# 24 of the 32 tiles of each up projection as seven block products, and plain f through DRAM

## The chip, the cores and the metric

The kernel runs on one core of one Trainium2 chip. The metric is device time in microseconds of one execution. A core has TensorE (PE, matmuls, with PEld loading its weights), VectorE (DVE), ScalarE (ACT), GpSimd (POOL) and SyncE (SP), which here only issues DMAs. Each works through its instructions in order and waits on semaphores. SBUF is the on-chip memory, PSUM holds what PE writes, and DRAM is reached by DMA.

## The reference

Two layers, each a token mixer (differential attention in layer 0, a gated short convolution in layer 1) and an MLP with squared ReLU, every part between two RMSNorms with gains, over 1024 tokens and 16 meta tokens of width 1024, in fp32. What the change touches is the MLP (D_MODEL 1024, D_FF 4096):

```python
def _sqrelu_mlp(h, w_up, w_down):
    a = jax.nn.relu(jnp.einsum('bld,df->blf', h, w_up))
    return jnp.einsum('blf,fd->bld', a * a, w_down)

def reference(...):
    ...
        hres = hres + _rmsnorm(m, norm_g[i, 1])
        h = _rmsnorm(hres, norm_g[i, 2])
        hres = hres + _rmsnorm(_sqrelu_mlp(h, w_up[i], w_down[i]), norm_g[i, 3])
    return hres[:, N_META:]
```

## The kernel before

Activations lie transposed: 128 features on the partitions, tokens along the row (1028 in layer 0, as four meta tokens are still needed there, and 1024 in layer 1). Every fp32 operand is split into a high part of reduced precision (`hi`, a cast on ACT) and the rest (`lo`, a subtraction on DVE), and every product is three matmuls: hi by hi, lo by hi, hi by lo. A weight tile of 128 outputs is one DMA of 512 KB into `w_raw`, then a cast and a subtraction of 128x1024 (`load_weights`, L149 and L150). With K = 1024 a tile takes 8 x 3 = 24 matmuls for each chunk of tokens (`product`, L187): three chunks of 340 to 344 in layer 0, two of 512 in layer 1.

The MLP of a layer runs in `mlp`. The first four up tiles (the head) run while the norm ahead of them is being finished: `norm_step` adds the residual into m (L389, L390), writes m to DRAM (L394), splits gain times m into H and L, and sums squares into ssn (ACT L211, POOL L212); a sum over the partitions on PE (L203) and `rsqrt_mean` then make the scale rs for each chunk. The up products run on the unscaled x and are scaled behind the ReLU (L456). Then come 24 tiles in twelve pairs (`up_pair`), and four plain tiles. f is the squared result. The down projection takes the 24 middle tiles of f by Strassen's scheme in Winograd's form: a 2 by 2 block product by seven products instead of eight. Its operand sums of f are made behind each pair (L486 to L489, on DVE), split, and written to `seven_dram` by two large DMAs (L494).

The head's f goes to `plain_dram` and comes back last. The last four plain tiles stay in SBUF in `stage`, and the down projection begins with them (`down_plain`, four weight tiles of two outputs each, ACT copying each result into acc). Meanwhile the first block of sums, fourteen loads of 514 KB, comes into the tiles that held H and L (the base load, L523). Then `Sevens.run` takes the seven products of each weight block in an order written out by hand for PE, three PSUM chains a, b and c, each product read out by a DVE add while the next ones run (L591, L614).

Only PE's order in the loops of seven is fixed by hand. Elsewhere the order on each engine and on SP's queue is made by a scheduler when the program is built, and then fixed. Tiles named by a tag share buffers: a new one waits until the old one's readers are done. The DMA semaphores are eight, used in turn, so that at most eight DMAs are under way. `wp` holds one `w_raw` and two pairs of hi and lo; `two` gives the two big tiles that hold v (a pair's f and sums) and later acc.

Of the kernel before, what the change touches and what calls it, by code (L numbers as in the profile page):

```python
# [16 lines left out]
F32 = mybir.dt.float32  # L17
F32R = mybir.dt.float32r
AF = mybir.ActivationFunctionType
ALU = mybir.AluOpType  # L20
# [62 lines left out]
def trunk(ctx: ExitStack, tc: tile.TileContext, xt, wall, gains, lam_p, subln, convw, out):  # L83
# [27 lines left out]
    plain_dram = [drp.tile([P, 2 * FB, w], F32, name=f"plain_dram{i}") for i, w in enumerate((T1, SEQ))]  # L111
# [335 lines left out]
    def up_product(fp, w, hi, lo, rs, cols, boundary=False):  # L447
        c0, n = cols
        ps = any_bank("up")[:, :n]
        if boundary:  # L450
            settle(0, cols)
        product(ps, w, hi, lo, 0, range(KC), cols)
        if boundary:
            settle(1, cols)
        r = fp.tile([P, n], F32, tag="r", name=f"r_{count[0]}", bufs=2)
        nc.vector.scalar_tensor_tensor(r, ps, 0.0, rs[:, c0 : c0 + n], ALU.max, ALU.mult)  # L456
        return r

    def up_plain(fp, hi, lo, rs, W, stage, groups, chunks, boundary=False):

        fh, fl = quarters(stage, W)
        for group in groups:
            ws = [weights() for _ in group]
            for cols in chunks:
                s = slice(cols[0], cols[0] + cols[1])
                for i, w in zip(group, ws):
                    r = up_product(fp, w, hi, lo, rs, cols, boundary)
                    nc.scalar.activation(r, r, AF.Square)
                    nc.vector.tensor_copy(fh[:, i, s], r)
                    nc.vector.tensor_sub(fl[:, i, s], r, fh[:, i, s].bitcast(F32))  # L470
                    spent(3 * KC, cols[1])

    def up_pair(fp, hi, lo, rs, H, t, chunks, stage, spool):

        v = flat(t)[:, : 8 * H].rearrange("p (a b) -> p a b", a=8)
        for e in range(2):
            w = weights()
            for cols in chunks:
                c0, n = cols
                r = up_product(fp, w, hi, lo, rs, cols)  # L480
                for z in range(2):
                    a, b = max(c0, z * H), min(c0 + n, (z + 1) * H)
                    if a < b:
                        nc.scalar.activation(v[:, SLOT[e, z], a - z * H : b - z * H], r[:, a - c0 : b - c0], AF.Square)
                spent(3 * KC, n)
        nc.vector.tensor_sub(v[:, 3], v[:, 7], v[:, 0])  # L486
        nc.vector.tensor_sub(v[:, 2], v[:, 5], v[:, 3])
        nc.vector.tensor_sub(v[:, 4], v[:, 5], v[:, 7])
        nc.vector.tensor_sub(v[:, 6], v[:, 1], v[:, 2])  # L489
        sv = stage[:, : 14 * H].rearrange("p (a b c) -> p a b c", a=7, b=2)  # L490
        for a, b in ((0, 4), (4, 7)):
            nc.scalar.copy(sv[:, a:b, 0], v[:, a:b])
            nc.vector.tensor_sub(sv[:, a:b, 1], v[:, a:b], sv[:, a:b, 0].bitcast(F32))
            nc.sync.dma_start(spool[:, a:b], sv[:, a:b].bitcast(F32))  # L494
# [150 lines left out]
    def mlp(layer, hi, lo, rs, H, two, base, base_plain, head, chunks, opened, psum_of, reopen):  # L645
# [3 lines left out]
        ff = ExitStack()  # L649
        fp = ff.enter_context(pool("ff", side="right"))  # L650

        def stage():
            return fp.tile([P, 2 * FB * W], F32R, tag="stage", name=f"stage{layer}_{count[0]}")

        st = stage()
        up_plain(fp, hi, lo, rs, W, st, [list(range(FB))], head, True)
        for i, f in enumerate(quarters(st, W)):
            nc.sync.dma_start(plain[:, i * FB : (i + 1) * FB], f.bitcast(F32))
# [739 lines left out]
```

## Time and profile before

| | us |
|---|---|
| time, median of 3 runs (lowest, highest) | 2402.52 (2401.92, 2403.31) |
| the profiled execution's own time | 2403.25 |
| its span | 2401.1 |
| granted TensorE clock over the span | 0.993 |
| PE without a matmul (span less busy) | 58.9 |
| layer 0: up from 606 to 980, plain down to 1025, down by sevens to 1265 | 374, 45, 240 |
| layer 1: up from 1689 to 2055, plain down to 2099, down by sevens to 2339 | 366, 44, 240 |

Matmuls overlap each other, so the length of one is more than its share of PE's time: 128x512 lasts 392 ns in the median while one starts every 229 ns. What a matmul costs is read from the pitch of a stretch, not from its duration.

### The profile page before, as it was taken

To read this page: it belongs to the slowest core of one execution; us is meant where nothing else is said; L and a number is where in the kernel's file an instruction comes from. 1 tells how busy PE (TensorE), PEld (TensorE's weight loads), DVE (VectorE), ACT (ScalarE), POOL (GpSimd) and SP (SyncE) were. 2 spreads that over 40 slices of the span, in tenths; PEclk is the share of its full clock that TensorE was granted. 3 is DMA by queue.
4 is the path that set the end of the run, shared out by engine and by line. 5 is a ranking of instruction groups with operands and counts; after the bars stand their busy time and mean duration, and the time that the engine had idled before them with its cause. 6 is when DMAs were issued, how large, how long until landed. Compare 5 with 4: busy or idle time off the path is not lost.

```text
span 2401.1 us, 36496 instructions
## 1 busy us (share of the span) xinstructions
PE 2342.2 (98%) x14330; PEld 2202.7 (92%) x14330; DVE 1485.9 (62%) x2663; ACT 996.4 (41%) x1901; POOL 445.3 (19%) x438
## 2 busy tenths in 40 slices
PE   8999999999999999999999999999999999999997
PEld 7899999999899999999999899999888888888886
DVE  7887777764954554367666944433954455277766
ACT  6777777765533333322224522224533333312224
POOL 3211111104400000033324200003400000133316
PEclk9999999999999999999999999999999999999998
DMA  4222222243355655475732411122355655477552
GB/s 136 58 63 62 63 63 63 74 144 113 108 212 203 234 190 207 176 291 206 270 136 97 139 45 47 51 68 61 119 219 202 228 218 185 177 288 261 214 200 71
DMA packets 109915, 357.66 MB, mean 149 GB/s; under 512 B 10928, under 2 KB 55344, under 8 KB 102576
## 3 DMA queue, kind: packets, MB, share of 16 engines
q1 hardware_dynamic: 109744, 355.33, 41.8%
q8 instruction: 113, 1.85, 0.3%
q14 instruction: 58, 0.48, 0.1%
HBM read 225.94 MB, written 120.84 MB: 144 GB/s over the span
## 4 chain that ended last, share of the span: by engine, by line
PE 81%; DVE 11%; ACT 3%; issue 2%; DMA 2%; SPq 0%; DVEq 0%; ACTq 0%
PE up L187 27%; PE pa L591 11%; PE dn L187 5%; PE pb L591 5%; PE mo L187 4%; PE bg L187 4%; PE ug L187 3%; PE cg L187 3%; PE pc L591 3%; PE po L1305 2%; DVE HL L392 2%; PE s L1219 1%; PE tr L1266 1%; PE s L1220 1%; PE q L972 1%
## 5 line engine op out<-in xcount | busy, mean ns | idle before, releaser
L187 PE MATMUL up<-HL,w_hi 128*128 128x344 f32 (+3 forms) x1312 | 453.8, 346 | 4.0 <-DVE HL L392 3.8
L187 PEld LDWEIGHTS up<-HL,w_hi 128*128 128x128 f32 x1312 | 247.0, 188 | 27.1 <-DVE HL L392 6.7
L150 DVE TENSOR_TENSOR w_lo<-w_raw,w_hi 128x1024 fp32r<-128x1024 f32 (+1 forms) x111 | 137.2, 1237 | 189.0 <-ACT w_hi L149 188.9
L456 DVE SCALAR_TENSOR_TENSOR r<-up,ssn 128x344 f32<-128x344 f32 (+3 forms) x164 | 93.5, 573 | 259.1 <-PE up L187 258.5
L149 ACT CAST w_hi<-w_raw 128x1024 fp32r<-128x1024 f32 (+2 forms) x135 | 140.3, 1040 | 260.2 <-PE up L187 153.5
L187 PE MATMUL up<-HH,w_hi 128*128 128x344 f32 (+1 forms) x768 | 246.0, 320 | 0.0
L187 PE MATMUL up<-HH,w_lo 128*128 128x344 f32 (+1 forms) x768 | 245.6, 321 | 0.0
L569 POOL TENSOR_TENSOR s_tmp<-w_raw 128x256 f32<-128x256 f32 x48 | 35.5, 739 | 1025.2 <-DMA w_raw<-in_wall 792.6
L187 PEld LDWEIGHTS up<-HH,w_lo 128*128 128x128 f32 x768 | 144.7, 189 | 0.5 <-issue 0.2
L187 PEld LDWEIGHTS up<-HH,w_hi 128*128 128x128 f32 x768 | 144.7, 188 | 0.2
L212 POOL TENSOR_TENSOR mss<-mss,sq 128x344 f32<-128x344 f32 (+2 forms) x42 | 50.1, 1198 | 375.8 <-ACT sq L211 366.8
L561 ACT CAST s_hi<-s_tmp 128x1024 fp32r<-128x1024 f32 x48 | 50.4, 1050 | 163.8 <-PE pb L591 147.0
L1229 ACT ACTIVATE E<-E,mn 16x16 f32<-16x16 f32 (+5 forms) x144 | 105.3, 732 | 23.9 <-DVE mn L1224 23.4
L187 PE MATMUL up<-YHb,w_hi 128*128 128x512 f32 (+2 forms) x272 | 103.6, 381 | 0.0
L187 PE MATMUL up<-YHa,w_lo 128*128 128x512 f32 (+2 forms) x272 | 103.6, 381 | 0.0
L187 PE MATMUL up<-YHb,w_lo 128*128 128x512 f32 (+2 forms) x272 | 103.5, 381 | 0.0
L187 PE MATMUL up<-YHa,w_hi 128*128 128x512 f32 (+2 forms) x272 | 103.4, 381 | 0.0
L187 PE MATMUL mo<-HL,w_hi 128*128 128x342 f32 (+2 forms) x312 | 99.9, 320 | 0.0
L150 POOL TENSOR_TENSOR w_lo<-w_raw,w_hi 128x1024 fp32r<-128x1024 f32 (+1 forms) x24 | 57.5, 2394 | 196.7 <-ACT w_hi L149 174.1
L1224 DVE CUSTOM_DVE_ANT_0 E<-s,G 16x16 f32<-16x16 f32 (+5 forms) x144 | 64.4, 455 | 39.9 <-PE s L1220 37.4
L614 DVE TENSOR_TENSOR acc<-acc,pa 128x512 f32<-128x512 f32 x96 | 65.8, 687 | 33.6 <-PE pa L591 32.0
L561 ACT CAST a_hi<-w_raw 128x512 fp32r<-128x512 f32 x48 | 29.8, 620 | 134.2 <-DMA w_raw<-in_wall 126.8
(501 smaller groups left out, 7291.4 us busy)
## 6 DMA issues: line engine op xcount, KB each, us to landing
w_raw<-in_wall SPq DMA_DIRECT2D x189, 512.0 KB, 3.7
seven_dram<-stage SPq DMA_DIRECT2D x12, 2056.0 KB, 6.3
seven_dram<-stage SPq DMA_DIRECT2D x12, 2048.0 KB, 6.3
fx<-seven_dram SPq DMA_DIRECT2D x42, 514.0 KB, 7.0
fx<-seven_dram SPq DMA_DIRECT2D x42, 512.0 KB, 6.9
seven_dram<-stage SPq DMA_DIRECT2D x12, 1542.0 KB, 9.3
seven_dram<-stage SPq DMA_DIRECT2D x12, 1536.0 KB, 8.7
HL<-seven_dram SPq DMA_DIRECT2D x21, 514.0 KB, 7.4
```

Source lines behind the costliest of these rows:

```text
L149: nc.scalar.copy(hi_part, raw[:, cols])
L150: (eng or nc.vector).tensor_sub(lo_part, raw[:, cols], hi_part.bitcast(F32))
L187: nc.tensor.matmul(ps, lhs[:, a:b], rhs(k, cols), start=n == 0, stop=n == last)
L212: (eng or nc.gpsimd).tensor_add(ss, ss, sq)
L392: nc.vector.scalar_tensor_tensor(row(L, c, s), mc, gn, hc.bitcast(F32), ALU.mult, ALU.subtract)
L456: nc.vector.scalar_tensor_tensor(r, ps, 0.0, rs[:, c0 : c0 + n], ALU.max, ALU.mult)
L561: nc.scalar.copy(hl[0], src)
L591: nc.tensor.matmul(ps[:, off : off + n], lhs[:, a : a + P], F[j][slot][:, t, c : c + n], start=first and k == 0, stop=k == 5, skip_group_c ...
L614: nc.vector.tensor_add(am, am, got)
L1224: nc.vector.tensor_tensor_reduce(out=e[:rows, p0 : p0 + n], in0=ps[:rows], in1=self.G[:rows, off : off + n], scale=-(2.0 ** -(h + 1)), sca ...
L1229: nc.scalar.activation(e[:rows, :ext], e[:rows, :ext], AF.Exp, scale=-1.0, bias=mn, accum_out=H["sums"][:rows, c : c + 1])
L1305: nc.tensor.matmul(po[:, a0:ncols], v[:, j], a[:, j, a0:ncols], start=j == 0 and z == 0, stop=j == nch - 1 and z == 2)
```

## The change

The 24 middle tiles of each up projection are computed by Strassen's scheme too: K is halved into even and odd groups of 128 features, the tokens into two halves of H = 514 or 512, the outputs into the two tiles of a pair. A pair is then seven products of 4 x 3 matmuls over one half of the tokens (in layer 0 two matmuls for each, of 258 and 256 columns). Their operands are four-term sums of x, made once for each layer on POOL from gain times m (`turn`: scaling on ACT, `sums` on POOL, split by `put`), and sums of weights, made on POOL for each pair (`combine`). Slots 3, 2 and 6 have operand tiles of their own (`x2`, `x1`); slots 0, 1, 5 and 4 use H and L, slot 4 after being overwritten. A pair's f and its four sums (now on POOL) go to `seven_dram` slot by slot, hi through a ring of four tiles, lo straight from v: fourteen DMAs of 263 KB.

All eight plain tiles come first. Their f goes to `plain_dram` chunk by chunk through small rings. The second four are loaded back into the buffer of `x2` when the pairs are done. The PSUM stage of the down projection opens ahead of the pairs.

```diff
-    plain_dram = [drp.tile([P, 2 * FB, w], F32, name=f"plain_dram{i}") for i, w in enumerate((T1, SEQ))]
+    plain_dram = [[drp.tile([P, 2 * FB, w], F32, name=f"plain_dram{i}_{j}") for j in range(2)]
+                  for i, w in enumerate((T1, SEQ))]
...
+    def up_plain(tp, hi, lo, rs, plain, groups, chunks, bufs, boundary=False, between=lambda i: None):
...
+                    r, fh = bufs()
+                    r, fh = r[:, :n], fh[:, :n]
+                    nc.vector.scalar_tensor_tensor(r, ps, 0.0, rs[:, s], ALU.max, ALU.mult)
+                    nc.scalar.activation(r, r, AF.Square)
+                    nc.vector.tensor_copy(fh, r)
+                    nc.vector.tensor_sub(r.bitcast(F32R), r, fh.bitcast(F32))
+                    nc.sync.dma_start(plain[:, i, s], fh.bitcast(F32))
+                    nc.sync.dma_start(plain[:, FB + i, s], r)
...
+    class UpSevens:
...
+        def turn(self, m, j, which):
+            for odd in range(2):
+                x = row(m, 2 * j + odd, slice(0, 2 * self.H))
+                nc.scalar.activation(x, x, AF.Copy, scale=gain(which[0], which[1], 2 * j + odd))
+            t1, t3, t4, t2 = self.halves(m, j)
+            sums(nc.gpsimd, t1, t3, t4, t2)
+            for slot, x in ((3, t1), (2, t2), (6, t4)):
+                self.put(slot, j, x)
...
+        def finish(self, q):
...
+            nc.gpsimd.tensor_sub(v[3], v[7], v[0])
+            nc.gpsimd.tensor_sub(v[2], v[5], v[3])
+            nc.gpsimd.tensor_sub(v[4], v[5], v[7])
+            nc.gpsimd.tensor_sub(v[6], v[1], v[2])
+            for slot in (0, 3, 5, 4, 2, 1, 6):
+                hi = self.fp.tile([P, H], F32R, tag="hi", name=f"fhi{q}_{slot}_{count[0]}", bufs=4)
+                nc.scalar.copy(hi, v[slot])
+                nc.sync.dma_start(self.spool[q][:, slot, 0], hi.bitcast(F32))
+                nc.vector.tensor_sub(v[slot].bitcast(F32R), v[slot], hi.bitcast(F32))
+                nc.sync.dma_start(self.spool[q][:, slot, 1], v[slot])
...
+                for q in range(n + 1):
...
+                    step(4, q - 1)
+                    step(5, q - 1)
...
+                    step(1, q)
...
+                    step(6, q - 1)
...
+                    step(2, q)
+                    step(3, q)
...
+                    step(0, q + 1)
...
-        for j in range(2 * NW):
-            up_pair(fp, hi, lo, rs, H, two(j % 2, f"f{layer}_{j}"), chunks, stage(), spool[j])
-        st = stage()
-        up_plain(fp, hi, lo, rs, W, st, [[i] for i in range(FB)], chunks)
+        up_plain(fp, hi, lo, rs, plain[1], [[i] for i in range(FB)], chunks, ring,
+                 between=lambda j: up.turn(m, j, (layer, 2)))
+        up.begin()
+        for j in range(4):
+            up.put(4, j, up.halves(m, j)[1])
+        psum_stage(*psum_of)
+        up.run(m)
...
+        st = xp.tile([P, 2 * FB * W], F32R, tag="x2", name=f"stage{layer}")
+        f = quarters(st, W)
+        for c0, n in chunks:
+            for i in range(2):
+                s = slice(c0, c0 + n)
+                nc.sync.dma_start(f[i][:, :, s].bitcast(F32), plain[1][:, i * FB : (i + 1) * FB, s])
```

Products 0, 2 and 3 are copied out of PSUM by ACT. Products 1, 4 and 5 are added to those copies by DVE, and the ReLU with rs (DVE) and the square (ACT) follow; product 6 goes through its ReLU on DVE at once. Products 0, 2, 4 and 6 of a pair run on in one PSUM chain (a), 3 and 5 in another (b), so that 4 waits for the copy of 2, and 5 for that of 3.

In the orders, names have lost their running numbers where these add nothing. First SP's queue where the up projection of layer 0 ends. Before, the last base loads are followed at once by the next weights (`w_raw`; the first of these two is the third plain down tile):

```order
L523 DMA HL<-seven_dram_79 128x1028
L523 DMA HH<-seven_dram_79 128x1028
L523 DMA HL<-seven_dram_79 128x1028
L138 DMA w_raw_10899<-in_wall 128x1024
L138 DMA w_raw_10989<-in_wall 128x1024
```

Now the load of `stage` stands behind the writes of pair 10 (`fhi`, and `f_10a` for lo):

```order
L578 DMA seven_dram_81<-fhi_1_621_11340 128x514
L578 DMA seven_dram_81<-fhi_6_621_11345 128x514
L580 DMA seven_dram_81<-f_10a 128x514 x3
L578 DMA seven_dram_81<-fhi_0_622_11489 128x514
L835 DMA stage_11529<-plain_dram_1_78 128x4x344 x4
L835 DMA stage_11529<-plain_dram_1_78 128x4x340 x2
L676 DMA HH<-seven_dram_81 128x1028
```

and, eleven base loads on, the writes of pair 11 stand ahead of that same weight tile, now `w_raw_11732`:

```order
L580 DMA seven_dram_81<-f_11b 128x514
L578 DMA seven_dram_81<-fhi_3_622_11494 128x514
L578 DMA seven_dram_81<-fhi_5_622_11499 128x514
L578 DMA seven_dram_81<-fhi_4_622_11504 128x514
L676 DMA HL<-seven_dram_81 128x1028
L580 DMA seven_dram_81<-f_11b 128x514 x3
L578 DMA seven_dram_81<-fhi_2_622_11509 128x514
L580 DMA seven_dram_81<-f_11b 128x514
L676 DMA HH<-seven_dram_81 128x1028
L676 DMA HL<-seven_dram_81 128x1028
L139 DMA w_raw_11732<-in_wall 128x1024
```

So six loads and nine writes have come in ahead of it. Second, POOL at the head of layer 0. Before, the adds into ssn of the last chunk of tokens stand together:

```order
L212 TENSOR_TENSOR ssn_6834<-ssn_6834,sq_7543 128x340
L212 TENSOR_TENSOR ssn_6834<-ssn_6834,sq_7553 128x340
L212 TENSOR_TENSOR ssn_6834<-ssn_6834,sq_7560 128x340
L212 TENSOR_TENSOR ssn_6834<-ssn_6834,sq_7567 128x340
L212 TENSOR_TENSOR ssn_6834<-ssn_6834,sq_7574 128x340
```

Now the sums of x (L475 to L478, on m0a and m0b) stand among them:

```order
L475 TENSOR_TENSOR m0a<-m0a 128x514
L476 TENSOR_TENSOR m0a<-m0a 128x514
L475 TENSOR_TENSOR m0a<-m0a 128x514
L213 TENSOR_TENSOR ssn_6836<-ssn_6836,sq_7562 128x340
L477 TENSOR_TENSOR m0a<-m0a 128x514
L476 TENSOR_TENSOR m0a<-m0a 128x514
L475 TENSOR_TENSOR m0b<-m0b 128x514
L213 TENSOR_TENSOR ssn_6836<-ssn_6836,sq_7569 128x340
```

Four more stand ahead of the last add. Third, ACT in the loop of pairs, here with the hi casts of pair 5 (`fhi` and the slot) between the copies of products 2 and 3 of pair 6 (`ua`, `ub`). Before, a pair's sums were cast by two instructions:

```order
L484 ACTIVATE f_4a<-r_8918 128x174
L149 CAST w_hi_9055<-w_raw_9053 128x1024
L484 ACTIVATE f_4a<-r_8947 128x340
L492 CAST stage_598_8767<-f_4a 128x4x514
L492 CAST stage_598_8767<-f_4a 128x3x514
```

```order
L577 CAST fhi_3_606_10071<-f_5b 128x514
L577 CAST fhi_5_606_10076<-f_5b 128x514
L588 ACTIVATE f_6a<-f_6a 128x514
L607 ACTIVATE f_5b<-f_5b 128x514
L577 CAST fhi_4_606_10081<-f_5b 128x514
L603 COPY f_6a<-ua_9917 128x514
L577 CAST fhi_2_606_10086<-f_5b 128x514
L577 CAST fhi_1_606_10091<-f_5b 128x514
L577 CAST fhi_6_606_10096<-f_5b 128x514
L603 COPY f_6a<-ub_10138 128x514
L577 CAST fhi_0_609_10317<-f_6a 128x514
```

The copies that free PSUM for products 4 and 5 now stand among casts that wait for POOL's sums and for ring tiles whose writes have landed.

More of the change, by code (lines that the diff above doesn't have):

```diff
@@ L445, in quarters @@
         return [t[:, i * FB * W : (i + 1) * FB * W].rearrange("p (a b) -> p a b", a=FB) for i in range(2)]
[L447 to L457, printed above, removed]
@@ L473, in up_pair @@
[L473 to L477, printed above, removed]
+            between(group[0])
             for cols in chunks:
                 c0, n = cols
[L480 to L494, printed above, removed]
+                s = slice(c0, c0 + n)
+                for i, w in zip(group, ws):
+                    ps = any_bank("up")[:, :n]
+                    if boundary:
+                        settle(0, cols)
+                    product(ps, w, hi, lo, 0, range(KC), cols)
+                    if boundary:
+                        settle(1, cols)
+                    r, fh = bufs()
[6 more added lines that the diff above has]
+                    nc.sync.dma_start(plain[:, FB + i, s], r)
+                    spent(3 * KC, n)
@@ L643, in run, with mlp, few @@
                     step(0, q + 1)
-    def mlp(layer, hi, lo, rs, H, two, base, base_plain, head, chunks, opened, psum_of, reopen):
+    def mlp(layer, mp, m, hi, lo, HL2, rs, H, two, base, base_plain, head, chunks, opened, psum_of, reopen):
         W, spool, plain = 2 * H, seven_dram[layer], plain_dram[layer]
[L649 to L653, printed above, removed]
-        st = stage()
-        up_plain(fp, hi, lo, rs, W, st, [list(range(FB))], head, True)
-        for i, f in enumerate(quarters(st, W)):
-            nc.sync.dma_start(plain[:, i * FB : (i + 1) * FB], f.bitcast(F32))
+        def few():
+            return [mp.tile([P, head[0][1]], d, tag=t, name=f"{t}_{count[0]}", bufs=4) for d, t in ((F32, "fr"), (F32R, "fh"))]
+        up_plain(mp, hi, lo, rs, plain[0], [list(range(FB))], head, few, True)
         opened.close()
@@ L672, in mlp @@
         for g in range(FB):
-            down_plain(acc, *quarters(st, W), [g], chunks, lambda mi, cols, am, ps: nc.scalar.copy(am, ps))
+            down_plain(acc, *f, [g], chunks, lambda mi, cols, am, ps: nc.scalar.copy(am, ps))
         seven.fetch(0)
@@ L821, in trunk @@
             [sevens(HL, h)[:, k] for k in range(7)]]
-    acc, last, ws, _ = mlp(1, yh, yl, ssn, h, two1, base, last_quarters(*YH, SEQ), fine, cut1, third,
+    acc, last, ws, _ = mlp(1, mp, m, yh, yl, (YH, YLq), ssn, h, two1, base, last_quarters(*YH, SEQ), fine, cut1, third,
                     ("psp3", {"a": 3, "b": 2, "c": 2, "o": 1}, 512, ["a", "b", "c", "a", "b", "c", "a"], "o"), lambda: None)
@@ L1365, in mlp @@
         blocks = [seven(FB * (b + 1)) for b in range(NW)]
-        return [full(w_up[layer]), plain(NF - FB), *blocks, plain(0)]
+        up = full(w_up[layer])
+        pairs = up[FB : NF - FB].reshape(-1, P, KC // 2, 2, P).transpose(0, 1, 3, 2, 4).reshape(-1, P, D)
+        return [up[:FB], up[NF - FB :], pairs, plain(NF - FB), *blocks, plain(0)]
     q, k, v = (full(w_in[0][:, n * D : (n + 1) * D]) for n in range(3))
```

150 lines of the change are left out of this document (136 added, 14 removed).

## The prediction

> **What bounds the kernel now.** The page comes first, for the span and the busy shares.
>
> ```profile
> span 2401.1 us, 36496 instructions
> PE 2342.2 (98%) x14330; PEld 2202.7 (92%) x14330; DVE 1485.9 (62%) x2663; ACT 996.4 (41%) x1901; POOL 445.3 (19%) x438
> PE 81%; DVE 11%; ACT 3%; issue 2%; DMA 2%; SPq 0%; DVEq 0%; ACTq 0%
> ```
>
> PE is busy for 98% of the span and carries 81% of the chain that ended last; only 58.9 us are left without a matmul. So matmul columns taken away are worth their whole time, as long as nothing else comes late. Next the chain in order of time (start, length, work) around both up projections, with the pitch of the pair loop by one DVE operation that runs once in each pair, and a stretch of the second up projection by windows (length, PE busy and its matmuls, clock, DMA share, GB/s).
>
> ```profile
> 653.28 327.02 PE up L187 x2081
> 980.31 45.08 PE dn L187 x288
> 1031.43 2.88 PE pa L591 x24
> 1041.46 2.88 PE pa L591 x24
> 2159.67 2.81 PE pa L591 x12
> 2169.47 2.81 PE pa L591 x12
> 1740.00:2040.00 300.00, 300.00 (x1308) 1.00 0.56 211
> L488 DVE TENSOR_TENSOR f_0a<-f_0a x1: 690/690/690, 688.8 to 688.8; 128x514 f32<-128x514 f32 x1
> L488 DVE TENSOR_TENSOR f_11b<-f_11b x1: 687/687/687, 937.8 to 937.8; 128x514 f32<-128x514 f32 x1
> ```
>
> The first up projection runs without a gap from 653 to 980, then the down projection's plain part follows at once. There are two prices of a Strassen matmul here already: the down loop's pitch is 10.03 us for 84 matmuls of 257 columns in layer 0 (0.1194 each) and 9.80 us for 42 of 512 in layer 1 (0.2333).
>
> **The columns that go.** Before, a pair of up tiles takes (937.8 - 688.8)/11 = 22.64 us in layer 0, and in layer 1 96 matmuls of 300.00/1308 = 0.2294, 22.02 us. After, a pair is 7 products: in layer 0 each 12 x 2 matmuls of 258 and 256 columns, 168 x 0.1194 = 20.06 us; in layer 1 12 of 512, 84 x 0.2333 = 19.60. Twelve pairs each: 12 x 2.58 = 31.0 and 12 x 2.42 = 29.0, so **-60 us**. The eight plain tiles of each layer cost PE the same as before.
>
> **The work beside a pair.** It must fit into 20.06 (19.60) us. DVE, ACT and POOL by shape:
>
> ```profile
> L614 DVE TENSOR_TENSOR acc0a<-acc0a,pa 128x514 f32<-128x514 f32 x48 | 33.1, 689 | 16.3 <-PE pa L591 15.7
> L562 DVE TENSOR_TENSOR s_lo<-s_tmp,s_hi 128x1024 fp32r<-128x1024 f32 x48 | 58.8, 1225 | 19.4 <-ACT s_hi L561 19.4
> L484 ACT ACTIVATE f<-r 128x512 f32<-128x512 f32 x48 | 30.4, 633 | 78.8 <-DVE r L456 78.8
> L561 ACT CAST s_hi<-s_tmp 128x1024 fp32r<-128x1024 f32 x48 | 50.4, 1050 | 163.8 <-PE pb L591 147.0
> L569 POOL TENSOR_TENSOR s_tmp<-w_raw 128x256 f32<-128x256 f32 x48 | 35.5, 739 | 1025.2 <-DMA w_raw<-in_wall 792.6 <-DVE s_lo L562 225.3 <-DVE acc L614 7.2
> L150 POOL TENSOR_TENSOR w_lo<-w_raw,w_hi 128x1024 fp32r<-128x1024 f32 x21 | 51.1, 2433 | 180.0 <-ACT w_hi L149 167.4 <-PE po L1305 12.6
> ```
>
> ACT: 14 operations of 514 (three PSUM copies, four squares, seven hi casts) at 0.63 and splits of three times 1.05 and once 0.62: 12.6 us. DVE: 14 of 514 (three adds and a ReLU from PSUM, three ReLUs and seven lo parts in SBUF) at 0.69, splits 3 x 1.23 + 0.69: 14.0 us. POOL: eight of 512 to 514; its two rows give 2.2 ns a column, so 1.31 each, 10.5 us. DMA: 14 x 263 KB written and 1.05 MB of weights read, 4.7 MB, 12.3 us at 385 GB/s (below). Each fits alone. DVE and POOL do not run freely beside each other, though (start, length):
>
> ```profile
> 642.91 2.92 DVE L392 SCALAR_TENSOR_TENSOR HL<-m0a,g,HH 128x340 fp32r<-128x340 f32 x3
> 649.64 1.53 DVE L392 SCALAR_TENSOR_TENSOR HL<-m0b,g,HH 128x340 fp32r<-128x340 f32 x3
> 643.39 5.53 POOL L212 TENSOR_TENSOR ssn<-ssn,sq 128x340 f32<-128x340 f32 x5 [0.60 <-ACT sq L211]
> ```
>
> The same three DVE operations take 2.92 us while POOL adds and 1.53 when it is idle, and the five adds 1.11 each where the slope gives 0.92. So a DVE operation and a POOL one of 340, 1.43 us alone, need 1.11 together: they take turns and hide 0.32. Of DVE's operations 14 have both inputs in SBUF (10 x 0.69 + 3 x 1.23 + 0.69 = 11.3 us); with POOL's 10.5 that is 21.8, less 8 x 0.32 = 19.2 us of 20.06 or 19.60. That is **96 to 98% full**, the tightest thing in the change. I walked one pair through the orders: product 4's add ends some 5 us ahead of product 6, the copies of products 2 and 3 about 3 us ahead of 4 and 5, the weights' low parts 4 to 6 us ahead. I take **+5 us** for both layers together, bounds 0 (all covered) and 47 (the second rival).
>
> The Trainium skill's page "SBUF — State Buffer", section "Who interferes with whom", has a rule against this change: a DVE instruction with two SBUF inputs and a GpSimd one that reads SBUF exclude each other for the whole instruction. The rows agree that they take turns, but the couple's 1.11 us is less than the 1.43 which whole instructions would need, so I keep the measured overlap; by the rule a pair is 21.8 us, not 20.06, and the sum is the second rival's.
>
> **The end of the up projection**, the price I expect. Before, the plain f is in SBUF when the down projection begins. Now it comes back from DRAM into the buffer of slots 3 and 2, behind pair 10's writes in SP's row, and the weights of the third plain down tile stand behind the fourteen base loads and most of pair 11's writes. DMA by windows, two issues of the base load on SP's queue, and issues by kind (size, us to landing):
>
> ```profile
> 984.00:988.00 4.00, 4.00 (x28) 1.00 1.03 417
> 996.00:1000.00 4.00, 4.00 (x27) 1.00 0.67 269
> 1000.00:1004.00 4.00, 4.00 (x28) 1.00 0.00 0
> 16.00:18.00 2.00, 2.00 (x14) 1.00 1.06 374
> 984.49 0.32 SPq L523 DMA_DIRECT2D HH<-seven_dram  x1
> 985.74 0.32 SPq L523 DMA_DIRECT2D HL<-seven_dram  x1
> w_raw<-in_wall SPq DMA_DIRECT2D x189, 512.0 KB, 3.7
> HL<-seven_dram SPq DMA_DIRECT2D x21, 514.0 KB, 7.4
> ```
>
> The base load fills the engines at 417 GB/s (rows of 4 KB) and is over by 999, 19 us into the plain part: that slack is what the change spends. SP issues one base load per 1.25 us, the time of its 514 KB, so what stands behind them is served behind them. Rows of 1.4 KB (x at the start) run at 374; for 2 KB I estimate 385. Clock from the end of product 6 of pair 10 in layer 0; a product is 20.06/7 = 2.87. Products 2 and 3 of pair 11 end at 5.7. No product 0 of a next pair stands between 3 and 4 here, so 4 waits for the copy of 2, which stands behind a hi cast of pair 10 on ACT: about 2 us (0 to 4). The last three low writes of pair 10 are ready near 9, and the stage loads go out behind them. Writes left 1.05 MB, 2.7 us; a third of the stage 1.4 MB, 3.8; signal 1.5 (w_raw's 3.7 less 1.3 for its 0.52 MB, less an issue): 17.0 against PE's 16.2, **1 us**. From 15.5, when that third is moved: the other two 7.5, base 7.2 MB 17.3, nine writes of pair 11 6.1, the weights 1.3 and 1.5, hi 1.05 and lo 1.23: 51.5. PE has done the first two weight tiles at 17.0 + 45.08/2 = 39.5: **12 us**. Behind the waiting cast on ACT stand only copies of products that need it. So 15 us in layer 0. In layer 1 a first chunk is 2.1 MB (3 us late) and the rest of the queue the same (9): 14. Together **+29**, bounds 3 (the weights come in time, only a first chunk is late) and 45 (8 us more each if all of pair 11's writes come first and run at half rate). The base load is complete near 46 and first read near 74, after the plain part: hidden, and one for one later if that cover went.
>
> **The start.** On POOL, ten operations of the four-term sums of x now stand among the last three adds into ssn (its rows are shown with the change): 10 x 1.31 = 13 us, 16 with DVE's turns. The sum on PE that needs the last add was at
>
> ```profile
> 652.55 0.73 PE L203 MATMUL sum<-ssn,minus 128*128 128x340 f32 x2
> ```
>
> 3.6 us behind the end of the adds (643.39 + 5.53), and now stands 95 matmuls of 0.157 (327.02/2081) later: 18.5 us to cover 13 to 16. The scalings of x on ACT (eight of 1028, some 1.1 us each by the 1.05 above) stand among the squares that feed those adds and wait for the residual's writes, which may use up the rest: **+4** for both layers, bounds 0 and 12. Ring waits of the plain tiles (two chunks in flight, each under 6 us of work and landing against 2 x 3.8 us of PE) cost nothing: PE's banks hide them; without that cover 1 to 2 us a chunk, up to 30 for all. The casts of X lie beside 4 x 11.3 us of plain tiles; later than those, they would be waited for one by one.
>
> **Sum:** 2403.25 (the profiled execution's own time, 0.7 above the median) - 60 + 5 + 29 + 4 = **2381 us**.
>
> **The rivals.** *The junction is covered.* The loads come in time: before, DMA was idle for much of the plain part's 45 us. Against it: 4.2 MB of stage and some 6 MB of writes are new in that stretch. 2403 - 60 + 3 + 4 + 2 = 2352; chance 0.13.
>
> *The turns of DVE and POOL bound the pair.* If nothing of a DVE and a POOL operation overlaps, a pair is 21.8 us: 12 x 1.7 + 12 x 2.2 = 47 us in place of my 5, so **2423**, slower than before. The place is the steady loop, with products 2 to 5 waiting for late copies and adds; it decides from (60 - 33)/24 = 1.1 us a pair on. For it: 96 to 98% full, with waits in order on four engines. Against it: the measured overlap of 0.32. Chance 0.22.
>
> *Half of that.* Pairs of 20.9, or the hi ring of four: the second cast that needs a written-out buffer stands ahead of the copy of product 2 on ACT, and 3.7 us of landing meet 3 us of slack. At 0.8 us a pair 2381 - 5 + 19 = 2395, up to 2410; chance 0.12.
>
> *That the change doesn't do what it says.* The new order has 144 matmuls more, as 288 more narrow ones in layer 0 and 144 fewer wide ones in layer 1 must give: out.
>
> **How the numbers follow.** Forecast (2362 to 2395) 0.53, covered 0.13, half 0.12, bound 0.22. To leave out no more than 0.2, the range runs from 2350 (the covered case) to 2420 (part of the bound one). Faster by over 0.2%, that is below 2397.7 (about what a measurement of this kernel can tell from no change): 0.53 + 0.13 + 0.06 = 0.72. Within it: 0.07. Slower: 0.21.
>
> **What would show it.** Right: a pair pitch of 20.1 and 19.6 us with PE full; one gap of some 10 us in each plain part, ended by the third weight tile, and a smaller one ahead of it that ends with the stage load. Wrong: a pitch over 21 with PE waiting for DVE or ACT (bound); no gap at the junction (covered); gaps over 5 us at the first sums of squares; ACT waiting for writes of hi in the steady loop (ring).

## The result and the profile after

The changed kernel takes 2465.24 us (median of 4 runs, 2462.77 to 2467.3) against 2402.22 (4 runs) for the kernel before on the same chip: a ratio of 1.0261, 95% interval 1.0243 to 1.0279. It is slower by 63 us where 21 less was forecast. The profiled execution's span is 2465.5 us.

The page of the changed kernel first, the span and the busy time of the engines:

```profile
span 2465.5 us, 38542 instructions
PE 2315.0 (94%) x14474; PEld 2162.6 (88%) x14474; DVE 1644.1 (67%) x2815; ACT 1114.4 (45%) x2141; POOL 771.0 (31%) x662
```

PE has 144 matmuls more and is busy for 27.2 us less (2342.2 before), not for 60 less, and the time without a matmul goes from 58.9 to 150.5 us. PE's waits that are new or longer are these (total, times, longest; the one for `HL` was 3.8 in all before):

```profile
PE dn L188 <- ACT w_hi L150: 19.7, 2, 11.5
PE ua L562 <- ACT f L603: 17.2, 11, 5.6
PE ua L562 <- DVE r L465: 10.1, 1, 10.1
PE up L188 <- DVE HL L393: 9.4, 12, 1.2
PE up L188 <- DVE w_lo L151: 5.9, 3, 3.6
PE ua L562 <- ACT fhi L577: 8.0, 6, 2.3
PE dn L188 <- DMA stage<-plain_dram: 4.6, 4, 1.8
```

They lie in three places: the plain down tiles (`dn`, L188), the pairs (`ua`, L562) and the eight plain up tiles ahead of them (L465, L393, L151). The pitch of the pairs, by the DVE operation that evacuates product 6 once in each pair (L606; first and last start):

```profile
L606 DVE SCALAR_TENSOR_TENSOR f_0a<-ua,ssn x1: 676/676/676, 757.4 to 757.4; 128x514 f32<-128x514 f32 x1
L606 DVE SCALAR_TENSOR_TENSOR f_10a<-ua,ssn x1: 680/680/680, 983.9 to 983.9; 128x514 f32<-128x514 f32 x1
L606 DVE SCALAR_TENSOR_TENSOR f<-ua,ssn x12: 676/678/691, 1863.4 to 2103.5; 128x512 f32<-128x512 f32 x12
```

In layer 0 ten pairs take (983.9 - 757.4)/10 = 22.65 us each, as many as a pair of plain tiles took before (22.64), where seven products are 20.06 us of matmuls. To see the stages apart, the table below takes their ends from the starts of PE's first matmuls of each kind (`up`, the first product, the first plain `dn`, the first `pa`); "pair" is the stage from the first product to the first plain down matmul over 12, so it holds the start and the end of the loop too.

| us, layer 0 / 1 | eight plain up tiles | pair | plain down | total |
|---|---|---|---|---|
| before | up projection 373.6 / 365.1 in all | | 45.1 / 44.8 | 2402.2 |
| after | 119.1 / 108.2 | 22.59 / 22.71 | 61.4 / 59.5 | 2465.2 |
| e1b_f_free | 119.0 / 109.0 | 21.18 / 20.94 | 62.3 / 58.8 | 2429.0 |
| e2_raw_once | 118.0 / 108.2 | 22.14 / 21.41 | 61.0 / 59.1 | 2445.9 |
| e3_both | 118.5 / 109.0 | 20.42 / 20.06 | 61.1 / 51.0 | 2399.3 |
| e4_no_pool_sums | 118.7 / 109.0 | 20.32 / 19.98 | 61.5 / 59.7 | 2407.9 |
| e5_sums_beside | 119.9 / 108.1 | 23.06 / 22.99 | 59.7 / 60.3 | 2477.9 |
| e6_sums_dve | 120.1 / 108.0 | 20.67 / 20.29 | 66.2 / 63.2 | 2424.5 |
| e16_comb_dve | 119.1 / 109.0 | 22.01 / 21.38 | 61.9 / 59.7 | 2444.3 |
| e7_ring4 | 111.8 / 109.2 | 22.62 / 22.13 | 62.3 / 58.2 | 2454.9 |
| e8j_base_later | 119.1 / 109.2 | 22.72 / 22.26 | 58.6 / 49.6 | 2458.0 |
| e17_base_last | 118.8 / 108.3 | 22.63 / 22.40 | 50.5 / 48.4 | 2460.0 |
| e8_three_fixes | 110.9 / 109.4 | 20.75 / 19.92 | 63.5 / 55.3 | 2402.1 |
| e9_split_ahead | 111.6 / 109.2 | 20.41 / 20.05 | 64.1 / 53.9 | 2402.3 |
| e10_x_sums_dve | 111.5 / 106.1 | 20.39 / 19.89 | 64.0 / 53.8 | 2396.8 |
| e14_all | 112.1 / 106.3 | 20.57 / 20.07 | 53.3 / 50.6 | 2401.1 |
| e18_down_order | 112.4 / 107.4 | 20.46 / 20.12 | 55.1 / 50.1 | 2386.5 |

The kernel before has no boundary between its plain tiles and its pairs: the eight tiles that stay plain are its up projection less twelve of its pairs, 373.6 - 12 x 22.64 = 101.9 and 365.1 - 12 x 22.02 = 100.9. So after against before: PE's columns -60.0 (by the two bare pitches), the pairs above those pitches 12 x 2.53 + 12 x 3.11 = +67.7, the eight plain tiles 17.2 + 7.3 = +24.5, the plain down part 16.3 + 14.7 = +31.0; together +63.2 of the 64.4 between the spans. Loops of pairs with the same code differ from one kernel to the next by up to 0.6 us a pair (22.13 to 22.71 in layer 1, over after, e7, e8j and e17), which is the grain of single runs. The totals of before, after, e14 and e18 are medians of several runs, the others one run each, beside a kernel before of 2408.4 (e2 to e4), 2407.5 (e1b, e5 to e7), 2401.7 (e8, e8j, e9, e10) and 2404.0 (e14, e16, e17) on the same chip; the eleven runs of e14 alone spread over 10 us. So the stages say more than small differences of totals. The first run of e1 had a granted clock of 0.556 throughout (a span of 3723.9 us); nothing is read from it.

What the pairs wait for is in two views. ACT's waits over nine pairs of layer 1 (1880 to 2080):

```profile
ACT us_hi L520 <- POOL t L535: 25.7, 6, 5.7
ACT f L603 <- DMA seven_dram<-fhi: 21.7, 4, 7.1
ACT f L603 <- DMA seven_dram<-f: 11.2, 4, 8.8
```

The chain that ended last, in the same stretch, from one split of `d` to the one after the next (start, length, work; the small issue pieces left out):

```profile
1957.37 0.60 DVE ud_lo L521
...
1958.29 4.42 DMA w_raw<-in_wall
...
1962.84 1.28 POOL t L534
...
1966.70 1.30 POOL t L537
...
1968.02 3.53 DMA w_raw<-in_wall
...
1971.62 1.06 ACT ua_hi L520
...
1976.60 0.60 DVE f L606
1977.20 0.60 DVE ud_lo L521
...
1978.26 5.80 DMA w_raw<-in_wall
...
1984.19 1.28 POOL t L534
...
1988.01 1.06 ACT us_hi L520
...
1999.13 0.60 DVE f L606
...
2002.61 0.60 DVE ud_lo L521
```

It is not PE's chain any more. It goes round through single buffers: the split of `d` frees the second raw half of the weights; its load takes 4.4 to 5.8 us; POOL combines; ACT and DVE split; DVE works off what has piled up behind that split in its order, up to the evacuation of product 6 and the next split of `d`. Two rounds take 2002.61 - 1957.37 = 45.2 us, 22.6 each. The wait of `f` (L603) belongs to a second round: product 0 is copied into a buffer that the pair two before has left, and that pair's low parts, which lie in it, must first land in DRAM. The view puts 21.7 us of this wait down to the writes of the high parts, which do not lie in that buffer; without the sending of the low parts all of it is gone (e1b, below). Both waits stand on ACT's one queue, and DVE waits for ACT's split behind them: in the first of the two rounds ACT waited 7.0 us for the writes and DVE then 4.9 us for the split, in the second ACT waited 5.7 us for the combination and DVE 6.0 for the split.

### The profile page after: what moved, and what is told of

Read it like the earlier page. It is cut to its first block, busy times and chain, and to the rows that moved or that the text cites. A ratio compares the mean times of both kernels' runs of the same rounds, so it can differ in the third digit from the quotient of the medians.

```text
span 2465.5 us, 38542 instructions
## 1 busy us (share of the span) xinstructions
PE 2315.0 (94%) x14474; PEld 2162.6 (88%) x14474; DVE 1644.1 (67%) x2815; ACT 1114.4 (45%) x2141; POOL 771.0 (31%) x662
## 5 line engine op out<-in xcount | busy, mean ns | idle before, releaser
L151 DVE TENSOR_TENSOR w_lo<-w_raw,w_hi 128x1024 fp32r<-128x1024 f32 (+1 forms) x63 | 82.6, 1313 | 153.1 <-ACT w_hi L150 153.0
L213 POOL TENSOR_TENSOR mss<-mss,sq 128x344 f32<-128x344 f32 (+2 forms) x42 | 50.1, 1197 | 375.8 <-ACT sq L212 372.6
L188 PE MATMUL up<-HL,w_hi 128*128 128x344 f32 (+3 forms) x352 | 120.9, 345 | 9.4 <-DVE HL L393 9.4
L521 DVE TENSOR_TENSOR us_lo<-t,us_hi 128x1024 fp32r<-128x1024 f32 x48 | 60.6, 1263 | 100.7 <-ACT us_hi L520 100.6
L151 POOL TENSOR_TENSOR w_lo<-w_raw,w_hi 128x1024 fp32r<-128x1024 f32 (+1 forms) x24 | 57.5, 2395 | 196.6 <-ACT w_hi L150 183.9
L188 PE MATMUL dn<-stage,w_hi 128*128 128x344 f32 (+2 forms) x320 | 91.0, 372 | 24.3 <-ACT w_hi L150 19.7
L188 PE MATMUL mo<-HL,w_hi 128*128 128x342 f32 (+2 forms) x312 | 99.9, 320 | 0.0
L1391 DVE CUSTOM_DVE_ANT_0 E<-s,G 16x16 f32<-16x16 f32 (+5 forms) x144 | 64.4, 455 | 39.9 <-PE s L1387 37.4
L188 PEld LDWEIGHTS dn<-stage,w_hi 128*128 128x128 f32 x320 | 61.5, 203 | 32.7 <-ACT w_hi L150 20.4
L579 DVE TENSOR_TENSOR f<-f,fhi 128x512 fp32r<-128x512 f32 x84 | 74.1, 931 | 22.7 <-ACT fhi L577 22.7
L188 PEld LDWEIGHTS up<-HL,w_hi 128*128 128x128 f32 x352 | 68.0, 193 | 16.4 <-DVE HL L393 13.0
L715 DVE TENSOR_TENSOR s_lo<-s_tmp,s_hi 128x1024 fp32r<-128x1024 f32 x48 | 58.8, 1224 | 23.6 <-ACT s_hi L714 23.6
L562 PE MATMUL ua<-x,us_hi 128*128 128x256 f32 (+2 forms) x288 | 67.2, 326 | 7.7 <-ACT us_hi L520 2.1
L520 ACT CAST us_hi<-t 128x1024 fp32r<-128x1024 f32 x48 | 50.1, 1046 | 52.5 <-POOL t L535 46.1
L1139 PE MATMUL q<-HH,w_hi 128*128 128x348 f32 (+1 forms) x192 | 65.1, 339 | 6.5 <-ACT w_hi L150 6.5
```

The lines of the kernel that those rows point to most:

```text
L151: (eng or nc.vector).tensor_sub(lo_part, raw[:, cols], hi_part.bitcast(F32))
L188: nc.tensor.matmul(ps, lhs[:, a:b], rhs(k, cols), start=n == 0, stop=n == last)
L521: nc.vector.tensor_sub(hl[1], src, hl[0].bitcast(F32))
L562: nc.tensor.matmul(ps[:, off : off + n], lhs[:, a : a + P], self.operand(slot, t, j)[:, c : c + n], start=first and k == 0, stop=k == 11, ...
L579: nc.vector.tensor_sub(v[slot].bitcast(F32R), v[slot], hi.bitcast(F32))
L1139: nc.tensor.matmul(ps, wh[:, a], self.HH[:, k, s], start=k == 0, stop=False)
```

## The experiments

**One wait, the other, both.** The theory was two such rounds of about equal length; the rival, that DVE and POOL are simply full, as they take turns. Three edits take away the wait for the writes, the wait for the load, and both.

```diff
 # e1, e1b, e3
-                nc.sync.dma_start(self.spool[q][:, slot, 1], v[slot])
+                nc.sync.dma_start(self.spool[q][:, slot, 1], hi.bitcast(F32))
 # e2, e3
         def fetch(self, q, half):
+            if q and half:
+                self.raw[q, half] = self.raw[0, half]
+                return
```

> The low parts of f of the pairs are not sent to DRAM: the hi part is sent twice, so the output is off and the bytes are the same. A pair's buffer is then free once its last low part is computed, not when its writes have landed. In the changed kernel the pairs take 270.8 us in layer 0 (727.3 to 998.0) and 272.5 in layer 1 (1831.8 to 2104.3), 22.6 and 22.7 each. Theory: two loops of about equal length close on ACT's queue, each some 13 us from product 6 to the next burst of splits: product 6, its sum, cast, low part and write, then the copy of product 0 into the same buffer (1976.53 to 1989.56); and the split of d, the load of the second raw half, the combination, the split of s21 (1977.13 to 1988.01). Cutting the first alone leaves the second: 22.0 to 22.6 a pair, total 2452 to 2465. Rival, turns of DVE and POOL bound the pair: no change, 22.6 and 22.7. Rival, the f buffer alone is the bound: 20.1 to 20.8 and 19.6 to 20.3, total near 2410.

> The same kernel as e1_f_free, whose profile shows a granted clock of 0.556 over the whole span and says nothing. The low parts of the pairs are not sent; the high part is sent twice. The run with both waits gone took 20.0 us a pair in layer 0, the one with the raw half loaded once 21.8. Theory of two loops: with the buffer of f free earlier the loop through the raw half remains, 21 to 22 us a pair, total 2430 to 2450. If the buffer of f alone is the bound: 20.1 a pair, total near 2405. Turns of DVE and POOL: 22.6, total 2465.

> The second raw half of the weights is loaded for the first pair only and used for all twelve, so the output is off; combination and splits are all done. Theory of two loops: the wait for the buffer of f stays, 22.0 to 22.6 us a pair, total 2450 to 2465. Rival, the raw half alone is the bound: 20.1 to 20.8 and 19.6 to 20.3 a pair, total near 2410. Rival, turns of DVE and POOL: no change.

> Both edits together (hi sent twice in place of hi and lo, second raw half loaded once). Theory of two loops: both waits of ACT are gone, 20.1 to 21.0 us a pair in layer 0 and 19.6 to 20.5 in layer 1, total 2402 to 2425. Rival, turns of DVE and POOL bound the pair: at least 21.8 in both layers, total over 2445.

Measured: 21.18 and 20.94 us a pair without the wait for the writes, 22.14 and 21.41 without the load, 20.42 and 20.06 without both. In us of pairs over both layers that is -38.3, -21.1 and -57.9: the two gains add up. Against the mean of the four kernels with unedited loops they are -35, -18 and -54, so the grain does not change the picture. One edit alone was worth more than two rounds of equal length allow (22.0 to 22.6 was at first expected of each), and the wait for the writes is the larger; with both gone the pair is where that theory had it. Two rounds side by side, of which only the longer counts, would not give gains that add up; two waits one behind the other on ACT's queue would. How far they are strung together was not taken apart further. ACT's waits in layer 1 show each edit doing what it should, one fence for each kernel; e1b keeps the wait for POOL's combination, e2 the one for the writes of f, and e3 has neither among its longer waits:

```profile
ACT us_hi L520 <- POOL t L535: 18.2, 8, 3.4
```

```profile
ACT f L606 <- DMA seven_dram<-f: 31.2, 7, 5.6
```

```profile
ACT f L610 <- DVE f L609: 20.2, 9, 2.2
```

In e3 all of DVE's, ACT's and POOL's work is there. Its pairs in layer 1 by windows (length, then busy time of PE, PEld, DVE, ACT and POOL, clock, DMA share, GB/s), and below it the changed kernel's:

```profile
1850.00:2020.00 170.00, 170.00 (x730) 136.09 (x729) 160.99 (x157) 97.79 (x156) 114.99 (x69) 1.00 0.61 221
```

```profile
1880.00:2080.00 200.00, 180.02 (x750) 138.68 (x749) 140.10 (x160) 100.79 (x160) 106.15 (x72) 1.00 0.62 213
```

In layer 0 e3's product 6 is evacuated at

```profile
L609 DVE SCALAR_TENSOR_TENSOR f_0a<-ua,ssn x1: 679/679/679, 757.1 to 757.1; 128x514 f32<-128x514 f32 x1
L609 DVE SCALAR_TENSOR_TENSOR f_10a<-ua,ssn x1: 678/678/678, 956.9 to 956.9; 128x514 f32<-128x514 f32 x1
```

that is 19.98 us a pair. PE is full, at 170.00/730 = 0.2329 a matmul in layer 1, while DVE is busy for 95% of the time. In the changed kernel DVE is busy for 70% and PE for 90%. So DVE and POOL together are nearly full, as the prediction said, and still fit: the amount of their work is not the bound.

**POOL's sums of f.** What do they do in these rounds? Left out, done beside the path, done on DVE:

```diff
 # e4, e5: the four slots take v[7]
-            nc.gpsimd.tensor_sub(v[3], v[7], v[0])
...
+                x = v[7] if slot in (2, 3, 4, 6) else v[slot]
 # e5: and the sums go to a dead row
+            nc.gpsimd.tensor_sub(spare, v[7], v[0])
...
 # e6
-            nc.gpsimd.tensor_sub(v[3], v[7], v[0])
+            nc.vector.tensor_sub(v[3], v[7], v[0])
```

> POOL's four sums of f of each pair are left out and the four slots made of them take the block in slot 7 in their place, so the output is off; casts, low parts and writes are as before. POOL keeps its four operations of the weights. Rival, turns of DVE and POOL bound the pair: POOL's share falls from 10.5 to 5.2 us, so the pair falls below 20.1 and 19.6 on this count and PE is full, total near 2405. Theory of two loops: the loop through f is 3 us shorter, the one through the raw half stays, 21.8 to 22.6 a pair, total 2445 to 2465.

> POOL's four sums of f are still done on the same inputs and at the same place in its queue, but their result goes to a row that nobody reads; the four slots take the block in slot 7, as in e4_no_pool_sums, so the output is off. So POOL's load on the buffers is that of the changed kernel, and only the casts no longer wait for POOL. Turns of DVE and POOL as the bound: back to 22 and more a pair, total 2440 to 2465. Length of the loops as the bound: near e4's 20.1 if the wait for POOL's sums on the way to the writes of f is what counted; 20.5 to 21.5 if part of e4's gain was that POOL reaches the weights earlier; total 2405 to 2430.

> The four sums of f on DVE in place of POOL, nothing left out. DVE's work is then 14.0 + 4 x 0.69 = 16.8 us of a pair and POOL's 5.2. Length of the loops: each sum costs 0.7 in place of 1.3 to 2.3 and DVE needs no hand-over, and POOL reaches the weights at once: 20.1 to 21.0 a pair, total 2405 to 2430. Turns of DVE and POOL: by whole turns 11.3 + 2.8 + 5.2 = 19.3 us, so also near 20.1. If DVE's own order is what decides, 21 to 22, total over 2430.

Without POOL's sums the pair falls to 20.32 and 19.98, against what the two rounds had led to expect: the turns count after all. With the sums back in POOL's queue, though no cast waits for them, it is 23.06 and 22.99, so the wait of the casts for the sums is not what counts. On DVE they give 20.67 and 20.29. The waits of the two rounds are still there in both short kernels, as ACT's longest wait over some nine pairs of layer 1 shows, for e4 and then e6:

```profile
ACT f L600 <- DMA seven_dram<-f: 36.8, 8, 6.3
```

```profile
ACT us_hi L520 <- POOL t L535: 27.9, 6, 5.1
```

So what e4 and e6 shorten is another piece of the rounds. DVE's seven low parts of a pair (xcount, busy, mean ns) in layer 1 for the changed kernel, e4, e5 and e3:

```profile
L579 DVE TENSOR_TENSOR f<-f,fhi 128x512 fp32r<-128x512 f32 x63 | 53.8, 903 | 0.0
```

```profile
L576 DVE TENSOR_TENSOR f<-f,fhi 128x512 fp32r<-128x512 f32 x63 | 40.9, 685 | 4.9 <-ACT fhi L574 4.9
```

```profile
L581 DVE TENSOR_TENSOR f<-f,fhi 128x512 fp32r<-128x512 f32 x63 | 58.4, 971 | 0.0
```

```profile
L582 DVE TENSOR_TENSOR f<-f,fhi 128x512 fp32r<-128x512 f32 x63 | 64.3, 1064 | 0.0
```

In e6 their mean is 685 ns again. POOL's sums stand beside DVE's busiest stretch, from the splits to the evacuation of product 6, and stretch these operations from 0.69 us to 0.9 and more on average. That makes both rounds longer. But in e3 they are stretched most, 1.06, and the pair is short, because nothing waits at the end of that stretch. So a slow stretch counts only as a piece of a round, and so does a wait: with either the waits gone (e3) or the stretching gone (e4, e6) the rest of the round fits into PE's time.

Whether the totals or the round decide was put to the test once more, with POOL's other job, the combination of the weights, moved to DVE. The totals of the two engines are then those of e6:

> Nothing left out: the changed kernel with POOL's other job on DVE in place of the sums of f: the four combinations of the weights. DVE's and POOL's totals are those of e6_sums_dve (16.8 and 5.2 us a pair). If the totals of DVE and POOL decide: pairs as in e6, 20.3 to 20.8 us, total 2420 to 2430. If the length of the chain decides, product 6, its evacuation among POOL's sums, the split of d, the load of the second raw half, the combination: POOL's sums still stand beside DVE's burst and DVE now waits for the load itself; 21.3 to 22.5, total 2440 to 2462.

22.01 and 21.38 us: the round, not the totals (e6 had 20.67 and 20.29). In e16 ACT's split still waits at the same point, now for DVE's combination behind the load:

```profile
ACT us_hi L520 <- DVE t L535: 29.9, 9, 7.9
```

**The plain up tiles.** The second four of them go to DRAM through two pairs of buffers; the edit lends them two more, of the weights' temporaries:

```diff
         def ring():
+            turn[0] += 1
+            if turn[0] % 4 < 2:
...
+            tags = [("t21", "s34_hi"), ("t34", "s34_lo")][turn[0] % 2]
+            return [wu.tile([P, 1024], d, tag=t, ..., bufs=1) for t, d in zip(tags, (F32, F32R))]
```

> Nothing left out: the second four plain up tiles cycle through four pairs of buffers in place of two (two of the ring and two of the weights' temporaries that are idle then). Theory: these tiles are held by the landing of their writes; PE's 10.1 us before the first pair in layer 0 fall to 0 to 4, and the plain part of both layers (119.4 and 108.2 us) by 7 to 15 in all, total 2450 to 2459. Rival, the work of DVE and ACT on the scaled x and the casts holds them: no change within 3 us.

PE's 10.1 us before the first pair fall to 2.2, and layer 0's plain part from 119.1 to 111.8. Layer 1's does not change (108.2, 109.2). So the wait for landing writes cost 7 us, in layer 0 alone.

**The junction.** First the base loads behind the weights of the third plain down tile in the program, then, with SP's queue held to the program's order, behind those of the fourth:

```diff
 # e17; e8j has g == 3 ahead of down_plain and no manual_schedule
-        for slot in range(7):
-            seven.load(0, slot)
...
+        with tc.manual_schedule(engines={mybir.EngineType.SP}):
+            for g in range(FB):
+                w = weights()
+                for slot in range(7) if g == FB - 1 else ():
+                    seven.load(0, slot)
```

> Nothing left out: in both junctions the fourteen base loads are issued behind the load of the third plain down tile's weights in place of ahead of it. In the changed kernel the plain down part takes 61.4 us in layer 0 and 59.5 in layer 1, with PE waiting 19.7 us for that tile's high part, against 45.1 and 44.8 of work. Theory (the third tile's weights stand behind the base loads): 48 to 52 us in each layer, total 2440 to 2450. Rival, the DMA engines are full there with stage, base and the last writes, so that something else is as late: 56 to 61, total over 2455.

> Nothing left out: the changed kernel with the order of loads of e14_all in the junctions and no other edit, to size that term alone. Plain down 61.4 and 59.5 us in the changed kernel, 45.1 and 44.8 of work. If the loads that stand ahead of the third and fourth tiles' weights are the term: 47 to 52 in both, total 2440 to 2450; if the stage load and the writes of pair 11 are: 54 to 60.

e8j mends layer 1 (49.6) and hardly layer 0 (58.6), where the fourth tile's weights are now behind the base loads. e17 has 50.5 and 48.4, 22 us less than the changed kernel, so the order of these loads is the term. But its total is only 5 less, 2460.0 where 2440 to 2450 was expected. PE's longest new wait in e17:

```profile
PE pa L744 <- ACT a_hi L714: 13.0, 3, 6.8
```

The gain is given back in the down loop: the fourteen loads of the second set of f now stand ahead of that loop's next weights, and the loops of seven take 251.7 and 249.9 us, against 242.3 and 239.7 in the changed kernel.

**All of it together.** e8 joins e6, e7 and e8j; e9 puts the split of `d` and the raw load ahead of the sums, casts and writes of f; e10 does the sums of x on DVE; e14 takes e17's order; e18 holds SP to the program's order in the down loop and spreads the second set's loads behind its weights.

> Nothing left out: sums of f on DVE (e6), four pairs of buffers for the second plain tiles (e7) and base loads behind the third weights (e8j) together. If the three act in stages of their own the gains add: pairs 248 and 244 us, plain 112 and 108, plain down 49 and 49: 2424.5 - 10 - 28 = 2386, range 2380 to 2400, below the kernel before. If the junction's gain is taken by pair 11's writes, which come faster: 2400 to 2412.

> e8_three_fixes, and the split of d and the load of the second raw half stand ahead of the sums, casts and writes of f in program order. If the loop through the raw half is what keeps the pair above PE's own time in e6 (20.7 and 20.3), the pairs fall to 20.1 to 20.4 and 19.6 to 20.0, 4 to 8 us below e8_three_fixes. If the writes of f are then later by as much, no change within 3 us.

> e9_split_ahead, and the sums of x at the start on DVE too, 16 of 0.7 us in place of 16 of 1.2 to 2.1 on POOL beside DVE's slowed operations. If POOL's sums among the last adds of ssn are what the start costs (plain part 111.8 in e7 against 102.3 for the same tiles before), 3 to 8 us less in layer 0; if the work of DVE itself is the limit there, no change or up to 5 us more.

> Nothing left out: e10_x_sums_dve, and in both junctions SP's queue keeps the program's order, with the fourteen base loads behind the weights of the fourth plain down tile. e10_x_sums_dve has pairs of 20.4 and 19.9 us, plain parts of 111.5 and 106.1 and plain down parts of 64.0 and 53.8 in 2396.8. If the base loads ahead of the fourth tile's weights are what the plain down part still waits for: 46 to 52 us in each layer, total 2375 to 2385, faster than the kernel before. If the stage load is the limit: 55 to 60 in layer 0, total 2388 to 2397.

> Nothing left out: e14_all, and SP's queue keeps the program's order in the down loop too, with the fourteen loads of the second set of f spread behind the weights of the loop's steps 2 to 4 in place of ahead of them. In e14_all PE waits 12.2 us for the first weights of the down loop, four times; e17_base_last won 22.0 us in the plain down parts and only 5.6 of 2465.5 in all. If that wait is what the new order of the base loads gave back, 8 to 14 us less than e14_all's 2401.1: 2387 to 2393. If the strict order makes later weights late: no change or more.

e8 came to 2402.1, outside its 2380 to 2400: its plain down part in layer 0, 63.5, is no shorter than without the edit (61.4). e9 changes nothing in the total (2402.3), and its pairs differ from e8's by less than the grain. e10 is 5 us lower, no more than single runs differ by; its plain part is 3 us shorter in layer 1 and the same in layer 0, where 3 to 8 were expected. The waits tell more. PE's waits for DVE's low parts of x (6.2 us for `HL` in e9) and of the weights (6.5 for `w_lo`) fall to 1.6 and nothing in e10, but a new one comes in; below it POOL's last two adds into `ssn` in layer 0 of e10:

```profile
PE sum L204 <- POOL ssn L213: 13.3, 2, 6.6
PE up L188 <- DVE HL L393: 1.6, 3, 0.8
```

```profile
655.04 13.97 POOL L213 TENSOR_TENSOR ssn<-ssn,sq 128x340 f32<-128x340 f32 x2 [1.54 <-ACT sq L212]
```

With the sums of x off POOL, DVE's low parts come in time. Instead, the first of these two adds lasts 13.0 us, where the add before it took 0.92: it ends when DVE's unbroken run of sums, casts and low parts ends (654.9 to 667.3). The sum over `ssn` on PE, which in e10's order stands behind 275 matmuls of the up projection and not behind 318, waits 6.6 us for it in each layer. So e10 took one wait away and brought another in.

e14, over 11 runs, is 2401.1 (ratio 0.999, 0.9981 to 0.9999), where 2375 to 2385 was expected: its plain down parts are 13.9 us shorter than e10's, but PE waits nearly as long as in e17 for weights early in the down loop:

```profile
PE pa L746 <- ACT a_hi L716: 12.2, 4, 5.2
```

e18, which cuts that wait to 2.2 us, is 2386.5 over 5 runs against 2402.93 (9 runs) for the kernel before: ratio 0.9929, 0.9916 to 0.9943, so 0.7% faster than the kernel before; its loops of seven are back at 242.2 and 240.3 us. The page's busy line of e18, and the two longest waits of PE that are left in the three places:

```profile
PE 2293.2 (96%) x14474; PEld 2152.9 (90%) x14474; DVE 1623.1 (68%) x2943; ACT 1112.1 (47%) x2141; POOL 604.2 (25%) x534
```

```profile
PE sum L204 <- POOL ssn L213: 12.8, 2, 6.6
...
PE dn L188 <- DMA stage<-plain_dram: 7.5, 3, 4.2
```

The first is the wait at the start of both up projections that came in with e10, the second the plain tiles' way back from DRAM.

## Why the prediction was wrong

*The columns* (-60) were right: 0.2329 a matmul in e3 where 0.2333 was taken, ten pairs in 199.8 us there where 200.6 was taken.

*The work beside a pair* (+5, bounds 0 and 47) is the step that failed: +67.7. The amounts of work were right, as was the point that DVE and POOL are nearly full, and e3 shows that they fit. What failed is the walk through one pair. It gave each item 3 to 6 us of slack against PE and did not follow the items round to their own beginning. With one buffer for the raw half, one for `d`, and two for f that are also the source of the writes, the next pair starts where this one ends, and the length of that round is a bound of its own: 22.6 us. Its pieces are the wait for the load and combination (21 us over both layers by e2), the wait for the writes of f (38 by e1b) and DVE's operations stretched by POOL's sums (e4, e6). Only the ring of the high parts was priced among the buffers; that the low parts lie in f itself and hold it until they have landed was not seen.

*The rival of the turns* (47 us, 2423) was nearer in amount and named waits for late copies, but its mechanism, that the sum of DVE's and POOL's work bounds the pair, falls with e3 and e16. What was right in it is that POOL's work slows DVE's, which counts as a piece of the round: taken off POOL, the sums of f give 20.67 and 20.29 us a pair. Its 2423 is still 42 us short, 21 of them in the pairs and most of the rest at the start. By the rule of the Trainium skill's "SBUF — State Buffer", "SBUF: two separate sides", that the one of the two engines that comes second is blocked for the whole instruction, a pair could not be under 21.8 us. e3's 20.0 with all the work in place does not agree with a sum of whole durations as the profile gives them, while the stretching from 0.69 to 1.06 us does agree that the two engines hinder each other.

*The end of the up projection* (+29) was right in size and cause: +31.0, with PE waiting 19.7 us for the third weight tile (12 + 9 were reckoned) and 4.6 for the stage loads (1 + 3); the rest of the 31.0 was not taken apart. e17 bears out the order of the loads as the cause. Not foreseen was that a better order there would show its price one stage later.

*The start* (+4) was too small: +24.5. The adds into `ssn`, which the prediction priced, were covered, as PE does not wait for them in the changed kernel. "Ring waits of the plain tiles cost nothing" was wrong in layer 0: 10.1 us of waiting, of which e7 takes 7.9. The term that was left out is that POOL's sums of x make DVE's low parts late: 5.6 us more of waiting for those of x (L393) and 5.9 for those of the weights (L151), and with the sums on DVE these two waits fall from 12.7 us (e9) to 1.6 (e10). Two low parts of x take 2.93 us in e9 beside POOL's sums and 1.04 in e10. The three waits together are 21.6 of the 24.5 us. Another 3.9 are PE's longer busy time in this stage, 195.8 us in both layers against 192.0 before, at a granted clock of 0.95 and 0.97 against 0.98 and 1.00. Other waits there are 1 us shorter.

## What to carry to other kernels

Work that fits each engine can still be too slow: follow the chain of one buffer through load, combination, split, use and release until it meets itself, add the lengths, and hold the sum against the pitch; in these runs the round got short either by taking its waits away or by moving the work that stretched its longest piece to another engine. Only the second was done with nothing left out (e6); a second buffer was not tried. A tile that is changed in place and then written out is held until the write has landed, and that belongs into the round. In one queue of loads, what is moved ahead can be paid by what stands behind (e17: 22 us won, 19.6 given back), so look one stage on before a reordering is called a gain.

## What the hardware showed that was not expected

A short POOL operation can be held for as long as DVE goes on without a break: the add of 128x340 in e10 above lasted 13.0 us in layer 0 and 12.95 in layer 1, beside 12 us of DVE operations end to end, and adds of the same shape took 0.92 to 1.24 just before. PE's wait for it shows that the delay is real, though the spans of POOL in a profile are rough.

After a gap PE comes back slowly. The end of layer 0's wait at the junction of the changed kernel by windows (columns as above):

```profile
1010.00:1020.00 10.00, 10.00 (x66) 10.00 (x65) 0.00 (x0) 2.12 (x5) 0.00 (x0) 1.00 1.02 408
1020.00:1030.00 10.00, 3.89 (x25) 3.60 (x24) 1.30 (x2) 2.37 (x5) 0.00 (x0) 0.91 1.05 364
1030.00:1040.00 10.00, 4.60 (x20) 4.60 (x21) 1.23 (x1) 1.04 (x1) 0.00 (x0) 0.57 0.78 300
1040.00:1050.00 10.00, 10.00 (x66) 10.00 (x65) 4.29 (x5) 4.73 (x10) 3.50 (x4) 1.00 0.17 55
```

The matmuls before the gap take 10.00/66 = 0.15 us, those right behind it 4.60/20 = 0.23 at a granted clock of 0.57. One by one (start, length), the slow ones are the first eleven: eight and three more up to the second line below, which begins 3.25 us behind the first.

```profile
1035.40 2.66 PE L188 MATMUL dn<-stage,w_hi 128*128 128x344 f32 x8 [11.51 <-ACT w_hi L150]
1038.65 0.32 PE L188 MATMUL dn<-stage,w_lo 128*128 128x344 f32 x1
```

That is 0.30 each, and at 0.15 they would have taken 1.7 us. So this gap of 11.5 us cost some 1.6 us beyond its length, and the mean clock of the span, 0.980 against 0.993 before, goes with the gaps. Over the whole span the trace's clock records grant half the clock during 62.7 us in which PE was busy, against 16.3 before. If half of that time is lost, an estimate, the difference is 23 of the 33 us by which PE's busy time fell short of the 60.
